# Strassen for the memory's values, with a summation tree, later hand-overs and gate tiles that leave the ring, in a one-core hybrid decoder layer

## The chip, the cores and the metric

The kernel runs on one core of one Trainium2 chip. The metric is the device time of one execution in microseconds (us). The engines are TensorE (PE, matrix products, with its weight loads listed as PEld), VectorE (DVE), ScalarE (ACT), GpSimd (POOL) and SyncE (SP), whose queue issues most of the DMAs. All weights come from HBM as float32 and the whole kernel keeps near-float32 accuracy.

## The reference

One layer works on x (256 tokens, width 2048) and a memory of 256 tokens:

```python
mem_h = rms_norm(mem, mem_norm_g)
x = x + hybrid_mixer(rms_norm(x, mix_norm_g), w_in, w_pool, ...)          # pooling heads and gated DeltaNet heads
x = x + memory_cross_attention(rms_norm(x, xa_norm_g), mem_h, w_xq, w_xkv, w_xo)
x = x + conv_glu_ffn(rms_norm(x, ffn_norm_g), w_gate, w_up, ...)          # width 5632
return rms_norm(x, final_norm_g)

def memory_cross_attention(h, mem_h, w_xq, w_xkv, w_xo):
    q = (h @ w_xq).reshape(B, S, XA_HEADS, XA_HEAD_DIM)
    kv = mem_h @ w_xkv                       # k: first 2048 columns, v: the other 2048
    s = einsum('bshd,bmhd->bhsm', q, k) * XA_HEAD_DIM ** -0.5
    o = einsum('bhsm,bmhd->bshd', softmax(s), v)
    return o @ w_xo
```

Inside the mixer, eight DeltaNet heads need per-token decays: the cumulative sums of g = -exp(a_log) * softplus(a + dt_bias), where a and b are 16 columns of the in-projection, scaled by the norm of x. The layer weights w_in, w_xkv, w_gate and so on are all 2048 rows deep, that is 16 tiles of 128 ("k tiles").

## The kernel before

**Products.** Every float32 operand is held as a pair: hi, a rounding that PE takes at full rate, and lo, the rest. One product of a weight tile with an activation tile is three matmuls, hi by hi, lo by hi and hi by lo. Weights come in raw tiles of 1 MB through a pool of three buffers (`load_raw`, tag raw, L110). Each raw tile is split in halves of 128x1024: a cast on ACT makes hi (L101), a subtraction on DVE makes lo (L102). The halves live in four buffers each (tags whi, wlo).

**Stages.** In the order of the program: the in-projection with the mixer's small products woven in; the keys of the memory (kk, w_k, 16 gemms); its values (pvs, w_v); the mixer's output (mix, w_mix); the queries (xq) with the attention; its output (xo); the feed-forward, whose gate and up products are done by Strassen's scheme in Winograd's form, on 11 blocks of four quarter products with 11 kinds of steps ("11", "22", "p1", "s3", ...); the down product; the last norm.

**Side lanes.** `job(lane, generator)` puts work in a lane; `pump` at set places of a gemm runs one step of a lane, up to the next `yield`; `drain` runs it to its end. So a `yield` is where PE goes on with gemm matmuls before the lane's next instruction. The lane "dn" first runs `decays`: it sums the logits (bc), transposes them (lps), scales them by the norm of x (rxps is the column sum of the squares xsum), makes gg, then gps (cumulative sums by matmul) and, in four quarters q, gm, its split gh and gl, and dps, the matmul whose exponential is the decay matrix Dm. The lane "dp" runs the four head pairs p (qp, w and others).

**The values.** `KV` holds keys and values. For each of four column groups n of 512, and for each of 16 k tiles, the memory's two token halves m_ (stationary mT, 128x128) are multiplied with the weight half (128x512 moving), three matmuls each, into two PSUM banks named pvs (L679 to L695). ACT scales the banks by the memory's norm rm on the way out.

**Gate and up.** `load`, `prepare`, `multiply` and `combine` (L979 on) work one step each: load one 512 KB tile, into the pool wr of eight buffers or, for the kind "11", into the SBUF region `ring`; split it; multiply; and combine PSUM banks. The load of "11" needs ring's space, which other tiles hold until the last xo product. A DMA on POOL's queue adds a second quarter onto the "11" tile, to give the sums s1, s2 and s4. While the first block runs, the lane "xr" transposes x (xtp) and writes it to DRAM (xt, xspill on SP's queue).

**Residual.** xres, x in its transposed form, is loaded in two DMAs of 1 MB (L703) and added to the mix banks (L706, L707).

**What sets the order.** A scheduler orders instructions on each engine by their place in the text and their priorities; the tiles of a pool decide when a load may be issued; a call of `seq` fixes the order of the instructions in it to that of the text.

## Time and profile before

| | |
|---|---|
| median of 3 runs | 1532.48 us (1530.06 to 1536.34) |
| profiled execution | 1533.36 us, of which the span is 1531.6 us |
| mean clock granted to PE | 0.992 |
| PE busy | 1490.8 us, 97% of the span, 7722 matmuls |
| DVE busy | 1099.3 us, 72% |
| ACT busy | 856.4 us, 56% |
| POOL busy | 221.5 us, 14% |
| chain that ended last | PE 82%, DVE 7%, DMA 4% |

The stages begin, in us of the span, at about: kk 313, values 412, mix 500, queries 588, attention output 705, gate and up 797, down 1275. Matmuls are pipelined, so the durations of neighbouring rows overlap, and the distance of their starts is what one costs. A number in brackets at the end of a row of a timeline is the idle time of the engine before the row and what ended it. PEclk is the granted clock of PE as a share of full speed.

### The profile page before, as it was taken

Reading aid. Unit: us, or ns where it says so; the run is one execution under the profiler, and the core shown is the slowest. Engines: PE = TensorE matmul, PEld = TensorE weight load, DVE = VectorE, ACT = ScalarE, POOL = GpSimd, SP = SyncE. Lnnn points to the kernel's source line nnn. Section 1 sums busy time; section 2 is a strip of 40 time slices with the busy share of each in tenths; the row PEclk is TensorE's granted clock in tenths of the full one; section 3 lists DMA queues with packets and bytes.
Section 4 is the critical chain, followed back from the end, with each engine's and each line's share of the span. In section 5 each row is a group of like instructions: output and inputs, shape, how many; then the busy total and the mean of one; then the engine's idle time right before and its main releaser. Section 6 shows DMA issues by size and latency. Waiting matters only on the chain.

```text
span 1531.6 us, 20542 instructions
## 1 busy us (share of the span) xinstructions
PE 1490.8 (97%) x7722; PEld 1261.1 (82%) x7722; DVE 1099.3 (72%) x1435; ACT 856.4 (56%) x1247; POOL 221.5 (14%) x237
## 2 busy tenths in 40 slices
PE   7899999999999999999988999999999999999997
PEld 4788889888888888998877888888888888888885
DVE  6978887676544676666756898898999998455445
ACT  5555656554444544555545666666666666444433
POOL 0442532441100121000320000000000000000000
PEclk9999999999999999999999999999999999999999
DMA  6445443457555555344539888888888879755651
GB/s 225 155 176 176 151 170 126 141 173 268 190 176 190 192 191 192 138 140 163 193 129 339 248 256 261 260 256 268 269 270 242 244 217 365 249 194 191 197 188 55
DMA packets 73715, 314.95 MB, mean 206 GB/s; under 512 B 12048, under 2 KB 12432, under 8 KB 57488
## 3 DMA queue, kind: packets, MB, share of 16 engines
q1 hardware_dynamic: 67136, 290.05, 54.1%
q0 software_dynamic: 6336, 23.07, 8.4%
q8 instruction: 60, 0.98, 0.2%
q10 hardware_dynamic: 144, 0.52, 0.1%
q14 instruction: 39, 0.32, 0.1%
HBM read 304.05 MB, written 9.57 MB: 205 GB/s over the span
## 4 chain that ended last, share of the span: by engine, by line
PE 82%; DVE 7%; DMA 4%; ACT 2%; POOL 2%; issue 1%; SPq 1%; POOLq 0%; ACTq 0%; DVEq 0%
PE b L882 9%; PE b L884 9%; PE b L883 9%; PE acc L1096 5%; PE acc L1095 5%; PE acc L1094 5%; PE xq L143 4%; PE xo L143 4%; PE mix L143 4%; PE kk L143 3%; PE pvs L691 2%; PE pvs L690 2%; PE pvs L689 2%; PE xq L144 2%; PE xo L144 2%; PE mix L144 2%
## 5 line engine op out<-in xcount | busy, mean ns | idle before, releaser
L960 ACT CAST wh<-wr 128x1024 fp32r<-128x1024 f32 x154 | 160.2, 1050 | 82.4 <-DVE wr L996 30.0
L961 DVE TENSOR_TENSOR wl<-wr,wh 128x1024 fp32r<-128x1024 f32 x154 | 185.2, 1219 | 27.1 <-ACT wh L960 26.0
L882 PE MATMUL b<-wh,hP 128*128 128x512 f32 x484 | 192.4, 398 | 8.0 <-ACT wh L960 5.5
L884 PE MATMUL b<-wh,hP 128*128 128x512 f32 x484 | 191.8, 397 | 0.0
L883 PE MATMUL b<-wl,hP 128*128 128x512 f32 x484 | 190.6, 394 | 1.0 <-DVE wl L961 1.0
L961 DVE TENSOR_TENSOR wl<-wd,wh 128x1024 fp32r<-128x1024 f32 x88 | 107.5, 1224 | 101.9 <-ACT wh L960 100.3
L960 ACT CAST wh<-wd 128x1024 fp32r<-128x1024 f32 x88 | 92.7, 1054 | 118.5 <-PE acc L1096 115.7
L961 DVE TENSOR_TENSOR wl<-ring,wh 128x1024 fp32r<-128x1024 f32 x88 | 106.5, 1220 | 31.9 <-ACT wh L960 31.8
L960 ACT CAST wh<-ring 128x1024 fp32r<-128x1024 f32 x88 | 91.5, 1051 | 63.5 <-PE b L884 24.8
L1094 PE MATMUL acc<-wh,aring 128*128 128x512 f32 x320 | 124.5, 389 | 0.0
L1095 PE MATMUL acc<-wl,aring 128*128 128x512 f32 x320 | 124.5, 389 | 0.0
L1096 PE MATMUL acc<-wh,aring 128*128 128x512 f32 x320 | 124.5, 389 | 0.0
L882 PEld LDWEIGHTS b<-wh,hP 128*128 128x128 f32 x484 | 91.9, 190 | 28.0 <-ACT wh L960 5.8
L102 DVE TENSOR_TENSOR wil<-wi,wih 128x1024 fp32r<-128x1024 f32 x78 | 100.3, 1293 | 16.1 <-ACT wih L101 15.8
L883 PEld LDWEIGHTS b<-wl,hP 128*128 128x128 f32 x484 | 91.9, 190 | 20.3 <-DVE wl L961 1.9
L884 PEld LDWEIGHTS b<-wh,hP 128*128 128x128 f32 x484 | 91.8, 190 | 18.8
L993 POOL DMA_DIRECT2D ring<-in_w_gu x44 | 38.5, 879 | 422.2 <-DVE sg L932 343.1
L101 ACT CAST wih<-wi 128x1024 fp32r<-128x1024 f32 x78 | 81.4, 1048 | 18.0 <-DMA wi<-in_w_in 6.3
L143 PE MATMUL xq<-h2T,wqh 128*128 128x512 f32 x240 | 84.9, 393 | 0.0
L143 PE MATMUL kk<-mT,wkh 128*128 128x512 f32 x240 | 84.4, 393 | 0.0
L143 PE MATMUL xo<-oT,woh 128*128 128x512 f32 x240 | 84.3, 392 | 0.0
L143 PE MATMUL mix<-yT,wmh 128*128 128x512 f32 x240 | 84.1, 392 | 0.0
(466 smaller groups left out, 3769.9 us busy)
## 6 DMA issues: line engine op xcount, KB each, us to landing
wr<-in_w_gu SPq DMA_DIRECT2D x156, 512.0 KB, 7.0
wd<-in_w_down SPq DMA_DIRECT2D x88, 512.0 KB, 4.8
wi<-in_w_in SPq DMA_DIRECT2D x39, 1024.0 KB, 5.0
ring<-in_w_gu POOLq DMA_DIRECT2D x44, 512.0 KB, 7.4
wk<-in_w_k SPq DMA_DIRECT2D x16, 1024.0 KB, 4.9
wv<-in_w_v SPq DMA_DIRECT2D x16, 1024.0 KB, 4.8
wm<-in_w_mix SPq DMA_DIRECT2D x16, 1024.0 KB, 4.9
wq<-in_w_xq SPq DMA_DIRECT2D x16, 1024.0 KB, 4.9
```

What stands on the lines that cost most here:

```text
L101: act.copy(hi, src)
L102: return dve.tensor_tensor(lo, src, hi.bitcast(F32), ALU.subtract)
L143: pe.matmul(ps, h, full, start=kk == 0, stop=False)
L144: i = pe.matmul(ps[:, T:], l, xt[:, 0, :], start=False, stop=False)
L882: pe.matmul(ps, xh, wh, start=first and i == 0, stop=False, skip_group_check=True)
L883: pe.matmul(ps, xh, wl, start=False, stop=False, skip_group_check=True)
L884: m = pe.matmul(ps, xl, wh, start=False, stop=last and i == 1, skip_group_check=True)
L960: cast[:] = [put(act.copy(h, src))]
L961: less[:] = [put(dve.tensor_tensor(l, src, h.bitcast(F32), ALU.subtract))]
L1094: pe.matmul(acc[t, n], ah, wh, start=first, stop=False)
L1095: pe.matmul(acc[t, n], ah, wl, start=False, stop=False)
L1096: return pe.matmul(acc[t, n], al, wh, start=False, stop=last)
```

## The change

It has five parts. The sum of x's squares is made by a tree of additions right behind the squares, in place of one reduction in the lane dn. Three hand-overs come later: dps yields 3, 2, 2 and 4 times in its four quarters in place of twice, and w of the first pair once more. The memory's sums for Strassen (`memory_sums`) are made in a lane during the K gemms 8 to 15, for half of the k tiles against the other half. The values are made by Strassen's scheme on column pairs c, in an order of steps that `seq` fixes in the text, with u and l tiles that serve two products each. In the feed-forward, the "11" tiles of the first block b = 0 come through the pool wr.

```diff
-            with tc.issue_after(last_split[0].ins):
-                dve.tensor_reduce(xsum, xsq.rearrange("p k t -> p t k"), AX.X, ALU.add)
+        for c in range(1, 4):
+            dve.tensor_tensor(xsq[:, 0:4], xsq[:, 0:4], xsq[:, 4 * c:4 * c + 4], ALU.add)
+        dve.tensor_tensor(xsq[:, 0:2], xsq[:, 0:2], xsq[:, 2:4], ALU.add)
+        dve.tensor_tensor(xsum, xsq[:, 0], xsq[:, 1], ALU.add)
...
-                yield
-                yield
+                for _ in range((3, 2, 2, 4)[q]):
+                    yield
                 dps = psd.tile([P, 512], F32, name="dps", tag="d")
...
+            if p == 0:
+                yield
             yield from more(2)
             w1 = psd.tile([P, 2, P], F32, name="w1", tag="d")
...
+        def memory_sums():
+            for g in range(2):
+                ...
+                dve.tensor_tensor(am, mg[:, :, 0].bitcast(F32), mg[:, :, 1].bitcast(F32), ALU.add)
+                yield
+                dve.tensor_tensor(s5, a21, a22, ALU.subtract)
+                dve.tensor_tensor(s7, a11, a21, ALU.subtract)
+                yield
+                dve.tensor_tensor(s6, a11, s5, ALU.subtract)
+                dve.tensor_tensor(s3, a12, s6, ALU.subtract)
+                yield
+                split(hi, lo, tmp[:, 1])
+                yield
...
+            up = ((("b3", A11), ("b2", A21)), (("b3", A12), ("b2", A22)))
+            low = ((("b1", A11), ("b7", A21)), (("b1", A12), ("b7", A22)))
+            one = lambda *u: (u, u)
+            KINDS = (("11", one(("b1", A11))), ("22", one(("b3", S3))), ("s1", one(("b5", S5))), ("u2", up),
+                     ("s3", one(("b7", S7))), ("u3", up), ("s2", one(("b6", S6))), ("21", one(("b1", A12))),
+                     ("l2", low), ("l3", low), ("s4", one(("b7", A22))))
+            loads = [(c, kind) for c in range(2) for kind in ("11", "22", "12", "u2", "u3", "21", "l2", "l3")]
...
+            def prepare(c, kind, h, uses):
+                two = slice(2 * h, 2 * h + 2)
+                ...
+                hi = st.tile([P, 2, 512], F32R, name="wvh", tag="whi", bufs=4)
+                lo = st.tile([P, 2, 512], F32R, name="wvl", tag="wlo", bufs=4)
+                seq(act.copy(hi, s))
+                seq(dve.tensor_tensor(lo, s, hi.bitcast(F32), ALU.subtract))
+                ready[c, kind, h] = hi, lo
+                if kind == "22":
+                    ...
+                    seq(dve.tensor_tensor(T4[c][:, two], raw[c, "11"][:, two], raw[c, "12"][:, two], ALU.add))
+                if kind == "s1":
+                    r = raw[c, "12"][:, two]
+                    seq(dve.tensor_tensor(r, r, raw[c, "22"][:, two], ALU.add))
+                if kind == "u2":
+                    r = T4[c][:, two]
+                    seq(dve.tensor_tensor(r, r, raw[c, "22"][:, two], ALU.add))
+                if kind == "s2":
+                    nc.gpsimd.dma_start(s, a["w_v"][2 * c, h][:, 2:4], accum_op=ALU.add)
...
+            AHEAD, NS, nl = 3, 22, 0
+            for s in range(-AHEAD, len(steps)):
+                while nl < len(loads) and due[loads[nl]] <= s + AHEAD + 10:
+                    fetch(*loads[nl])
+                    nl += 1
+                if s + AHEAD < len(steps):
+                    prepare(*steps[s + AHEAD])
+                if s < 0:
+                    continue
+                if s == NS + 1:
+                    last_part(0)
+                combine(s // NS, s % NS)
+                multiply(*steps[s])
+            last_part(1)
...
+            if f == 8:
+                for lane in ("dn", "dp", "pool"):
+                    drain(lane)
+                job("ms", memory_sums())
...
-        if kind == "11":
+        if kind == "11" and b:
             r = ring[:, 2 * (b % 2) + j].rearrange("p (i c) -> p i c", i=2)
         else:
             r = fp.tile([P, 2, 512], F32, name="wr", tag="wr", bufs=8)
```

`multiply` runs, for each use of a step's half tile, six matmuls of 128x512 (two k tiles by three); a step of the kinds u2, u3, l2 and l3 has two uses, one of the others one. `combine` and `last_part` form the values from the banks b1 to b7 with three DVE sums at step 14, three ACT scalings at 16, two DVE sums at 18, one ACT copy at 21, and one DVE sum behind the pair's end. `fetch` loads a u or l tile in one DMA of 1 MB and the others in two of 512 KB.

The first place is DVE's start: the splits of the first in_k weights (w0l, wil), the logits (bc), the sum of squares (xsum) and the norm (rxms). Before:

```order
L102 TENSOR_TENSOR w0l<-w_79,w0h 128x1024
L268 TENSOR_TENSOR bc<-bps,bc 16x256
L102 TENSOR_TENSOR wil<-wi,wih 128x1024 x2
L276 TENSOR_REDUCE xsum<-xsq 128x256
L102 TENSOR_TENSOR wil<-wi,wih 128x1024
L171 TENSOR_SCALAR rxms<-rxps 128x2
```

And now:

```order
L102 TENSOR_TENSOR w0l<-w_79,w0h 128x1024
L252 TENSOR_TENSOR xsq<-xsq 128x1024 x2
L272 TENSOR_TENSOR bc<-bps,bc 16x256
L252 TENSOR_TENSOR xsq<-xsq 128x1024
L253 TENSOR_TENSOR xsq<-xsq 128x512
L255 TENSOR_TENSOR xsum<-xsq 128x256
L102 TENSOR_TENSOR wil<-wi,wih 128x1024 x4
L171 TENSOR_SCALAR rxms<-rxps 128x2
```

The sum moved from behind two wil splits to before the first of them, and bc stands inside it.

The second place is SP's queue from the K weights (wk) over the values (wv), the mixer's output (wm), the queries (wq) and the attention's output (wo) to the first gate tiles (wr, ring), with the loads of xres and the writes of x (xspill). Before:

```order
L110 DMA wk<-in_w_k 128x2048 x9
L703 DMA xres<-in_xT 128x2048 x2
L110 DMA wk<-in_w_k 128x2048 x7
L110 DMA wv<-in_w_v 128x2048 x16
L110 DMA wm<-in_w_mix 128x2048 x16
L110 DMA wq<-in_w_xq 128x2048 x16
L110 DMA wo<-in_w_xo 128x2048 x16
L987 DMA ring<-in_w_gu 128x1024 x2
L987 DMA wr<-in_w_gu 128x1024 x10
L899 DMA xspill<-xt 128x512
```

And now, where the loads of the values at L743 are halves of 512 KB and those at L110 whole tiles (the middle of them left out):

```order
L110 DMA wk<-in_w_k 128x2048 x16
L743 DMA wv<-in_w_v 128x1024 x6
L110 DMA wv<-in_w_v 128x2048 x2
L743 DMA wv<-in_w_v 128x1024 x2
...
L110 DMA wm<-in_w_mix 128x2048 x4
L847 DMA xres<-in_xT 128x2048 x2
L110 DMA wm<-in_w_mix 128x2048 x12
L110 DMA wq<-in_w_xq 128x2048 x16
L110 DMA wo<-in_w_xo 128x2048 x16
L1131 DMA wr<-in_w_gu 128x1024 x9
L1131 DMA ring<-in_w_gu 128x1024
```

xres moved behind all of the values' loads, and the first gate tiles are wr's.

The third place is DVE at the start of the values: wvl are splits, vsum the sum of the tiles 11 and 12 (wv_4328 and wv_4334), wv_4331 the tile 22, wv_4337 the tile u2, km the last of the K gemms. Before, splits alone stood here; now:

```order
L759 TENSOR_TENSOR vsum_4353<-wv_4328,wv_4334 128x1024
L160 TENSOR_TENSOR km_4325<-kk_4290,kc_4323 128x256
L754 TENSOR_TENSOR wvl_4356<-wv_4331,wvh_4355 128x1024
L759 TENSOR_TENSOR vsum_4353<-wv_4328,wv_4334 128x1024
L754 TENSOR_TENSOR wvl_4371<-vsum_4353,wvh_4370 128x1024
L762 TENSOR_TENSOR wv_4334<-wv_4334,wv_4331 128x1024
L754 TENSOR_TENSOR wvl_4382<-vsum_4353,wvh_4381 128x1024
L762 TENSOR_TENSOR wv_4334<-wv_4334,wv_4331 128x1024
L754 TENSOR_TENSOR wvl_4396<-wv_4337,wvh_4395 128x1024
```

The second of the vsum rows from 11 and 12 is the last reader of the tile 11, and it stands behind the second split of 22 (wvl_4356); the first split of u2 (wvl_4396) is the last row.

## Rows read from the trace of the kernel before

**Rows 1.** The page, busy time by engine, share of the span, instructions.

```profile
PE 1490.8 (97%) x7722; PEld 1261.1 (82%) x7722; DVE 1099.3 (72%) x1435; ACT 856.4 (56%) x1247; POOL 221.5 (14%) x237
```

**Rows 2.** Waits of PE: line, releaser, us in total, times, longest us.

```profile
PE dps L324 <- ACT gh L101: 2.7, 3, 1.8
...
PE b L883 <- DVE wl L961: 1.0, 2, 0.5
```

**Rows 3.** Timeline of PE, 20 to 36 us: start, duration, [idle before <-releaser].

```profile
23.34 0.51 PE L143 MATMUL in_k<-hT,wih 128*128 128x512 f32 x1 [1.07 <-ACT wih L101]
24.60 0.58 PE L144 MATMUL in_k<-hT,wil 128*128 128x256 f32 x1 [0.75 <-DVE wil L102]
...
33.18 0.58 PE L166 MATMUL rxps<-cst,xsum 128*128 128x1 f32 x4 [0.81 <-DVE xsum L276]
34.22 0.39 PE L144 MATMUL in_k<-hT,wil 128*128 128x256 f32 x1 [0.46 <-DVE wil L102]
```

**Rows 4.** Busy time by windows; after POOL: PEclk, DMA share, GB/s.

```profile
25.00:28.00 3.00, 3.00 (x11) 2.52 (x11) 3.00 (x2) 1.96 (x2) 0.00 (x0) 0.51 0.85 289
33.00:40.00 7.00, 6.36 (x28) 5.57 (x29) 5.04 (x7) 1.69 (x4) 1.62 (x1) 0.76 0.51 177
797.00:804.00 7.00, 6.53 (x21) 4.70 (x22) 6.24 (x7) 5.88 (x8) 3.03 (x3) 0.59 1.00 351
840.00:844.00 4.00, 4.00 (x13) 3.10 (x12) 2.52 (x3) 2.11 (x3) 0.00 (x0) 0.57 1.03 410
```

**Rows 5.** Timeline of PE, the other idle places before it.

```profile
55.79 0.40 PE L311 MATMUL gps<-gg,cst 128*128 128x16 f32 x2 [1.94 <-DVE gg L304]
...
72.87 0.50 PE L324 MATMUL dps<-gh,mgr 128*128 128x512 f32 x1 [1.78 <-ACT gh L101]
...
153.10 1.13 PE L423 MATMUL qp<-Z,C 128*128 128x128 f32 x8 [2.50 <-DVE Z L418]
...
194.08 0.46 PE L529 MATMUL w<-R,Yall 128*128 128x128 f32 x2 [1.41 <-DVE R L522]
...
796.89 0.79 PE L882 MATMUL b<-wh,hP 128*128 128x512 f32 x1 [5.50 <-ACT wh L960]
...
808.46 0.66 PE L896 MATMUL xtp<-cst,xres 128*128 128x128 f32 x4 [1.66 <-ACT xt L898]
...
839.08 0.50 PE L882 MATMUL b<-wh,hP 128*128 128x512 f32 x1 [2.45 <-DVE ring L1019]
```

**Rows 6.** Timeline of DVE, 17 to 36 us.

```profile
19.93 0.41 DVE L268 TENSOR_TENSOR bc<-bps,bc 16x256 f32<-16x256 f32 x1 [2.07 <-ACT bc L267]
23.32 2.36 DVE L102 TENSOR_TENSOR wil<-wi,wih 128x1024 fp32r<-128x1024 f32 x2 [2.98 <-ACT wih L101]
25.59 7.44 DVE L276 TENSOR_REDUCE xsum<-xsq 128x256 f32<-128x4096 f32 x1
```

**Rows 7.** Timeline of PE in the values, seven steps from first to last.

```profile
439.77 0.39 PE L690 MATMUL pvs<-wvl,mT 128*128 128x512 f32 x1
...
441.40 0.40 PE L691 MATMUL pvs<-wvh,mT 128*128 128x512 f32 x1
```

**Rows 8.** Busy time by windows, K gemms and values: PE, PEld, DVE, ACT, POOL.

```profile
313.00:412.00 99.00, 98.64 (x573) 86.54 (x571) 64.25 (x90) 48.52 (x79) 25.47 (x28) 1.00 0.59 213
412.00:500.00 88.00, 88.00 (x380) 70.86 (x379) 39.42 (x33) 38.66 (x41) 0.00 (x0) 1.00 0.55 191
```

**Rows 9.** The tile wv: durations in ns (min, median, max), landing of its loads.

```profile
L101 ACT CAST wvh<-wv x32: 1035/1047/1057, 401.2 to 488.0; 128x1024 fp32r<-128x1024 f32 x32
L102 DVE TENSOR_TENSOR wvl<-wv,wvh x32: 1219/1224/1445, 402.3 to 489.1; 128x1024 fp32r<-128x1024 f32 x32
...
DMA to landing us min/median/max: 4.7/4.8/5.3
```

**Rows 10.** The tile xres: landing of its two loads.

```profile
DMA to landing us min/median/max: 7.9/9.0/10.1
```

**Rows 11.** Waits on SP's queue: line, releaser, us in total, times, longest us.

```profile
SPq L987 <- PE xo L141: 25.0, 1, 25.0
```

More of the change, by code (lines that the diff above doesn't have):

```diff
@@ L667, in hybrid_trunk @@
         mT = mbox[0]
+        mS = []
+        def memory_sums():
+            for g in range(2):
+                tmp = dn.tile([P, 2, 4, T], F32, name="mtmp", tag="kall", bufs=1)
+                if g:
+                    pair = dn.tile([P, 2, 4, T], F32R, name="mS1", tag="Yall", bufs=1)
+                    hi, lo = pair[:, 0], pair[:, 1]
+                else:
+                    hi, lo = (dn.tile([P, 4, T], F32R, name=n, tag="u4", bufs=2) for n in ("mSh", "mSl"))
+                mS.append((hi, lo))
+                am, ss = tmp[:, 0], tmp[:, 1].rearrange("p w (k t) -> p w k t", k=2)
+                mg = mT[:, 4 * g:4 * g + 4]
+                dve.tensor_tensor(am, mg[:, :, 0].bitcast(F32), mg[:, :, 1].bitcast(F32), ALU.add)
+                yield
+                a11, a12, a21, a22 = (am[:, k:k + 2, t * P:(t + 1) * P] for t in range(2) for k in (0, 2))
+                s5, s6, s7, s3 = (ss[:, w] for w in range(4))
+                dve.tensor_tensor(s5, a21, a22, ALU.subtract)
[6 more added lines that the diff above has]
+                yield
@@ L676, in hybrid_trunk @@
                 drain("mem")
+            if f == 8:
+                for lane in ("dn", "dp", "pool"):
+                    drain(lane)
+                job("ms", memory_sums())
             m = evac(ps, "k")
             pool.tensor_tensor(Kt[:, f, :], m, rmb, ALU.mult)
-        for n in range(4):
-            pvs = [psd.tile([P, 512], F32, name="pvs", tag="d") for _ in range(2)]
-            for kg in range(4):
-                raw = load_raw(a["w_v"][n, kg], [P, 4, 512], "wv")
-                gr = wsplit(raw, 2, "wv")
-                for k in range(4):
-                    kt = kg * 4 + k
-                    h, l = gr[k // 2][0][:, k % 2, :], gr[k // 2][1][:, k % 2, :]
-                    for m_ in range(2):
-                        s = slice(m_ * P, (m_ + 1) * P)
-                        pe.matmul(pvs[m_], mT[:, kt, 0, s], h, start=kt == 0, stop=False)
-                        pe.matmul(pvs[m_], mT[:, kt, 0, s], l, start=False, stop=False)
-                        i = pe.matmul(pvs[m_], mT[:, kt, 1, s], h, start=False, stop=kt == KT - 1)
-                    if kt % 2 == 1:
-                        pump(i)
-            for m_ in range(2):
-                act.activation(Vt[:, m_, n * 512:(n + 1) * 512], pvs[m_], AF.Copy, scale=rm[:, m_:m_ + 1])
+        drain("ms")
+        values()
         drain("dn")
```

73 lines of the change are left out of this document (added).

## The prediction

> **What bounds the kernel now.** I read the page first: TensorE (PE) is busy for 1490.8 of 1531.6 us, 97%, and DVE for 72% [rows 1]. So time falls only if PE gets fewer matmuls or loses less than the some 41 us that it stands idle or the extra that it spends at half clock. Next I read the list of what PE waited for: dps 2.7 us in three pieces, splits of gate weights (wl) 1.0 in two [rows 2]; none of the values' matmuls is in that list. Then the timeline of PE gave the other pieces where the change works: the sum of x's squares (rxps 0.81), gps 1.94, qp 2.50, w 1.41, and the entrance to the gate products, 5.50 for the first weight tile, 1.66 and 2.45 soon after [rows 3, 5]. A table by windows gave the granted clock behind them: 0.76 of full speed from 33 to 40 us, after the rxps wait, 0.59 for 7 us after the first gate tile, 0.57 for 4 us after the 2.45 [rows 4]. Full speed is the 2.4 GHz level; between that and 1 a window mixes it with 1.2 GHz. The profiled execution took 1533.36 us, 0.88 above the median 1532.48 and 1.76 beyond its span; the sum is made against it.
>
> **The sum of squares.** Before, one reduction of 128x4096 on DVE takes 7.44 us from 25.59, between the splits of the second weight tiles of in_k, and PE waits 0.81 for it at 33.18 and 0.46 for the split behind it at 34.22 [rows 3, 6]. The tree is three sums of 128x1024 (1.22 each, the median of a split of that shape [rows 9]), one of 512 (0.6, an estimate between its neighbours) and one of 256 (0.41 for 16x256, bc's row): 3.66+0.6+0.41 = 4.7 us. It stands before those splits, and DVE idles there 2.07 before 19.93 and 2.98 before 23.32, which is 5.05 in all [rows 6]: it fits, just. The two waits go, 1.27, and with them the slow stretch, 24% of the 7 us from 33 to 40, 1.7 [rows 4]. Together -3.0. If the tree ends a microsecond late, the 1.07 and 0.75 waits before it [rows 3] grow by that: bounds -3 to 0.
>
> **Hand-overs.** The dps matmuls come one step later in the first and two in the last quarter; they waited 2.7 for ACT's gh, the largest piece 1.78 before the last quarter [rows 2, 5], and PE has other gemm work in those steps, so about -2.7 at best; since the delay moves the later parts of the lane by three steps, some other wait may grow: -3 to -1. The w matmul of the first pair waited 1.41, and one step more takes it out: -1.4 [rows 5]. gps and qp, which waited 1.94 and 2.50 [rows 5], are moved against their producers by nothing that I can price: 0, bounds -2 to +3 by the larger of them.
>
> **Values, the work.** Before: 2 halves x 4 columns x 16 k x 3 = 384 matmuls of 128x512. They start every 0.233 us (439.77 to 441.40, seven intervals [rows 7]; the 392 to 399 ns of the group's rows overlap). After, per column pair 8 half-k kinds use one product (11, 22, s1, s3, s2, 21, s4) or two (u2, u3, l2, l3), 15 uses x 2 halves x 6 matmuls = 180, and two pairs: 360. That is -24 x 0.233 = -5.6 us. In exchange DVE gets 12 more splits at 1.22, 12 sums at about 1.22 and some ten combines of 128x512 at 0.6 to 0.7, together some 36 us, in a stage where it was busy 39.4 of 88 [rows 8]: it has room. ACT's 12 casts of 1.05 too.
>
> **Values, the waits.** The rows cannot show this, so I walk it through. A weight tile of 1 MB takes 4.7 to 5.3 us from issue to landing, median 4.8 [rows 9], and there are three raw buffers. Before, a tile lasted PE 24 x 0.233 = 5.6 us and two were ahead, so PE was never idle here, 88.0 busy of 88.0 [rows 8]. Now 11, 22 and 12 hold all three from the start, as each is needed for sums, and u2's load stands on SP behind the last sum 11+12. A single step is 6 x 0.233 = 1.40, a double one 2.80. Let 0 be PE's first step. The last split of 22 takes a wh buffer that the K gemm frees at 0, so cast 1.05, split 1.22 and sum 1.22 [rows 9] end at 3.5. u2 lands at 8.3 to 8.6, is cast by 9.6 and split by 10.8. PE wants it after six steps, at 8.4: it waits 1.2 for the cast and 0.9 for the split. u3 takes the buffer that u2 leaves at 13.1, lands at about 18 and is split at 20.3; PE wants it at 18.9: 1.1 more. The second pair has the same order, its sum about 0.6 later: 2.7 and 1.1. Together 2.1+1.1+2.7+1.1 = 7.0 us of new waits; bounds 0 (loads early or the buffer free sooner) and 14 (each tile late by its whole 4.8, less what lies between).
>
> Behind a wait the clock may fall. Of the waits of 1.4 us and over before, 2.50 and 2.45 were followed by slow stretches [rows 4, 5]; 1.94, 1.78, 1.66 and 1.41 were not. A stretch costs some 43% of 4 us, 1.7. I take two stretches and let half of the second be hidden in the next wait, +2.0; bounds 0 and 6.8. So the stage comes to -5.6+7.0+2.0 = +3.4. [...]
>
> **Sums for the memory, and xres.** The sums of the memory's tiles run in the K gemms f 8 to 15 on DVE, 8 us in a stage where DVE was busy 64 of 99 [rows 8]: 0, bounds 0 to 1. xres's two loads leave SP's queue behind wk's ninth and go behind wm's fourth, waiting for the values' last step; they take 7.9 to 10.1 us [rows 10] and the first residual can be late by some 16 us before a PSUM bank is missed (three of the 16 mix gemms, which last 88 us): 0, bounds 0 to +3.
>
> **Entrance to the gate.** Before, the first tiles go into the ring, whose space is free only when the last xo matmul is done; SP waited 25.0 us for it and issued the loads behind it [rows 11]. PE lost 5.50 until the cast, then 41% of 7 us, 2.9, to the clock; 1.0 for two splits; later 1.66 and 2.45, and 43% of 4, 1.7 [rows 2, 4, 5]: 15.2 in all. After, the first loads wait only for splits on DVE some 18 us earlier, so they land before xo ends. But the first gate product now takes the PSUM bank of the last xo gemm, and must wait for the second residual add of f 15, which stands behind a split on DVE: 0.4 for the matmul to end, two adds of 0.41 with a split of 1.22 between them, 2.4 us. Then one slow stretch, 1.7, and in the first block, where xt has two buffers and each waits for its spill's DMA in a full queue, waits such as 1.66, 2.45 and a split's 0.5 remain; I take 4.3 for them. Together 8.4 for 15.2: -6.8; bounds -11 (only 4.2 left) and 0 (the later tiles come as late as before, since the DMA engines were full, shares 1.00 and 1.03, in both windows there [rows 4]).
>
> **Sum.** -3.0-2.7-1.4+0+3.4+0-6.8 = -10.5: 1533.4-10.5 = 1522.9, against medians some 1522 to 1523.
>
> **The rivals.** (a) The values don't wait: loads land before they are wanted, as they did before. Against it: the chain sum, load, cast, split is 10.8 long and PE is there at 8.4. Then -5.6 in place of +3.4: 1514. (b) The entrance keeps its loss: the wait for the ring's space is replaced by that for the bank, and with the DMAs full to 844 every later tile arrives as before; only the stage at the start gains: 1533.4-7.1+3.4 = 1530. For it are the shares 1.00 and 1.03 [rows 4]; against it that the first 4 MB leave 18 us earlier. (c) Slower: in the values each wait for u2 and u3 lets the clock fall, and it stays at half through the double tile, 24 x 0.233 = 5.6 us more for each of the four, 22.4 in place of 2.0. That gives 1543. It decides if a wait of 1.1 us is enough to drop the clock and it comes back only after the tile. For it: 1.07 and 0.75 at 23 us were followed by 0.51 for 3 us [rows 3, 4]; against it: 1.94 and 1.78 were not followed by any.
>
> **How the numbers follow.** Forecast 0.53, its own range 1517 to 1529; (a) 0.13; (b) 0.21; (c) 0.13. A measurement of this kernel can tell about 0.5%, 7.7 us, from no change. Faster than 1524.8: two thirds of the forecast's chance, 0.35, and (a)'s 0.13, 0.48. Same: the rest of the forecast, 0.18, and (b), 0.39 less 0.01. Slower: (c), with a little of (b): 0.14. The range takes in (a)'s side and (b), and half of what lies to (c): 1512 to 1537.
>
> **What would show it.** In the profile after: no reduction of 7.44 us and no wait at rxps; dps not in PE's list, w shorter; 360 pvs matmuls; in that stage PE waits for the cast and split of the u tiles, four places, 7 us; first gate matmul some 2.4 us after the last of xo, waiting for DVE's residual. Wrong, if the values show no wait (a), if the clock is low through them (c), or if PE loses some 15 us between the end of xo and 54 us later (b).

## The result, and the profile after

The change is slower: 1544.34 us (1542.29 to 1544.89, 6 runs) against 1535.11 us for the kernel before in the same six rounds, ratio 1.0064 with a 95% interval of 1.0049 to 1.0079. The profiled execution has a span of 1542.6 us, 11.0 more than before.

The page of the kernel after, busy time by engine. To be read beside [rows 1]: PE has 24 matmuls less and 2.7 us less to do, and yet the span is longer, so PE waits some 14 us more.

```profile
PE 1488.1 (96%) x7698; PEld 1256.4 (81%) x7698; DVE 1136.5 (74%) x1487; ACT 871.6 (57%) x1263; POOL 221.8 (14%) x241
```

Where the time went is told by the first start of each stage's matmuls, from the rows of the tiles (us). By the same rows the attention's output begins at 696.1 in the kernel before, and the down product at 1280.0, not at about 705 and 1275.

| stage | before | after | length before | length after |
|---|---|---|---|---|
| in_k to its end | 13.3 to 77.7 | 11.6 to 74.7 | 64.4 | 63.1 |
| from there to the first kk | 315.2 | 323.5 | 237.5 | 248.8 |
| kk | 409.4 | 418.3 | 94.2 | 94.8 |
| values (pvs) | 499.0 | 512.4 | 89.6 | 94.1 |
| mix, queries, xo to the last xo | 791.0 | 804.3 | 292.0 | 291.9 |
| to the first gt (block 0 of gate and up) | 857.8 | 868.9 | 66.8 | 64.6 |
| from there to the first down product | 1280.0 | 1291.0 | 422.2 | 422.1 |

Two stages got longer: the second half of the mixer by 11.3 us, where the prediction had a gain, and the values by 4.5, where it had a loss of 3.4. The first gate block, where it had its largest gain, won 2.2.

The list of PE's waits after (line, releaser, us in total, times, longest us). rmpb, pool, ops, in_u and the second qp row are new against the list of before; dps is down from 2.7 [rows 2] to 0.8, with 0.5 more for gl, and the xsum row is gone, as forecast.

```profile
...
PE pvs L782 <- DVE wvl L754: 3.7, 5, 1.2
PE gps L313 <- DVE gg L306: 3.0, 1, 3.0
PE rmpb L180 <- DVE rmdg L177: 2.8, 1, 2.8
PE qp L425 <- DVE Z L420: 2.7, 1, 2.7
PE xtp L1040 <- ACT xt L1042: 2.5, 2, 1.6
PE b L1026 <- DVE ring L1163: 2.4, 1, 2.4
PE b L1026 <- DVE xres L851: 2.4, 1, 2.4
PE pool L143 <- DVE Dm L481: 2.1, 1, 2.1
PE qp L425 <- POOL C L418: 1.8, 1, 1.8
PE pvs L781 <- ACT wvh L753: 1.8, 2, 1.2
PE b L1026 <- ACT wh L1104: 1.7, 1, 1.7
PE ops L541 <- DVE vs L536: 1.6, 1, 1.6
PE in_u L144 <- DVE wil L102: 1.6, 1, 1.6
...
PE dps L326 <- ACT gh L101: 0.8, 1, 0.8
```

The timeline of DVE after, 286 to 315 us (start, duration, in brackets the idle time before and what ended it), shows where three of these come from. mt is the pooled mean of a feature tile; it waits for pB, POOL's shifted sums. Each time something that PE needs stands behind it on DVE's queue: vs for ops, two sums of the lane and a wil split for in_u, Dm for the pool product.

```profile
286.80 0.43 DVE L604 SCALAR_TENSOR_TENSOR mt<-pB,pA 128x256 f32<-128x256 f32 x1 [2.05 <-POOL pB L600]
...
287.23 0.35 DVE L536 TENSOR_SCALAR vs<-w,sbA 128x128 f32<-128x128 f32 x1
...
303.70 0.42 DVE L604 SCALAR_TENSOR_TENSOR mt<-pB,pA 128x256 f32<-128x256 f32 x1 [2.99 <-POOL pB L600]
...
305.00 1.22 DVE L102 TENSOR_TENSOR wil<-wi,wih 128x1024 fp32r<-128x1024 f32 x1
...
313.39 0.43 DVE L604 SCALAR_TENSOR_TENSOR mt<-pB,pA 128x256 f32<-128x256 f32 x1 [2.77 <-POOL pB L600]
...
313.81 0.69 DVE L481 TENSOR_TENSOR Dm<-raw_kq,Dm 128x512 f32<-128x512 f32 x1
```

In the kernel before the same waits stand in the timeline of DVE at 300 to 309 us, but what is behind them there (a split that was early, vs at 309) was not yet wanted:

```profile
300.66 0.43 DVE L600 SCALAR_TENSOR_TENSOR mt<-pB,pA 128x256 f32<-128x256 f32 x1 [1.35 <-POOL pB L596]
...
308.86 0.42 DVE L600 SCALAR_TENSOR_TENSOR mt<-pB,pA 128x256 f32<-128x256 f32 x1 [2.77 <-POOL pB L596]
```

rmpb is a matmul of the memory's norm: it wants DVE's rmdg, which wants POOL's rmr, which wants DVE's rmms. In the timeline of DVE after, rmms stands right behind f, an operation of the lane that waits for POOL, and the two pieces of rmdg take 1.48 us, beside C, an operation of the lane that the timeline of POOL has at that time:

```profile
221.72 0.16 DVE L550 TENSOR_TENSOR f<-sq__2299 128x4 f32<-128x4 f32 x1 [1.06 <-POOL sq__2299 L476]
221.80 0.16 DVE L171 TENSOR_SCALAR rmms<-msum 128x2 f32<-128x2 f32 x1
222.77 1.48 DVE L177 TENSOR_SCALAR rmdg<-cst,rmr 128x128 f32<-128x128 f32 x2 [0.81 <-POOL rmr L172]
```

```profile
222.71 1.26 POOL L418 TENSOR_TENSOR C<-U,cst 128x512 f32<-128x512 f32 x1
```

In the timeline of DVE before, no wait stands in front of rmms and rmdg takes 0.48, so 1.0 to 1.1 us each of rmpb's 2.80 come from these two neighbours:

```profile
226.32 0.13 DVE L171 TENSOR_SCALAR rmms<-msum 128x2 f32<-128x2 f32 x1
227.26 0.48 DVE L177 TENSOR_SCALAR rmdg<-cst,rmr 128x128 f32<-128x128 f32 x2 [0.81 <-POOL rmr L172]
```

In the values, the timeline of PE after shows the wait for u2 of the first column pair, and the slow matmuls behind it: starts 0.43 apart in place of 0.23 [rows 7], seven times up to 433.4, which is the 1.2 GHz level. It is the only slow stretch of that stage.

```profile
428.53 0.49 PE L781 MATMUL pvs<-wvh,mT 128*128 128x512 f32 x1 [1.21 <-ACT wvh L753]
429.79 0.49 PE L782 MATMUL pvs<-wvl,mT 128*128 128x512 f32 x1 [0.77 <-DVE wvl L754]
...
430.44 0.63 PE L781 MATMUL pvs<-wvh,mT 128*128 128x512 f32 x1
430.87 0.63 PE L782 MATMUL pvs<-wvl,mT 128*128 128x512 f32 x1
```

Between the starts 428.53 and 429.79 lie 1.26 us, where 0.23 is normal; the row names 0.77 as idle. So this wait cost 0.26 more than the bracket says, and some 0.1 at the next matmul; the others of the stage cost 0.16 to 0.27 more, and the same 0.1 where no second wait followed. The stage is 360 x 0.233 = 84 us of matmuls, nine waits of 6.0 us together, 2.5 for their restarts, and 1.6 for the slow stretch: the measured 94.1.

### The profile page after: what moved, and what is told of

Its sections match the earlier page's. It is cut to its first block, busy times and chain, and to the rows that moved or that the text cites. A ratio compares the mean times of both kernels' runs of the same rounds, so it can differ in the third digit from the quotient of the medians.

```text
span 1542.6 us, 20613 instructions
## 1 busy us (share of the span) xinstructions
PE 1488.1 (96%) x7698; PEld 1256.4 (81%) x7698; DVE 1136.5 (74%) x1487; ACT 871.6 (57%) x1263; POOL 221.8 (14%) x241
## 4 chain that ended last, share of the span: by engine, by line
PE 79%; DVE 9%; DMA 4%; ACT 3%; POOL 3%; issue 2%; SPq 0%; DVEq 0%; POOLq 0%; ACTq 0%
PE b L1026 9%; PE b L1027 9%; PE b L1028 9%; PE acc L1238 5%; PE acc L1239 5%; PE acc L1240 5%; PE xq L143 4%; PE kk L143 4%; PE mix L143 4%; PE xo L143 3%; DVE wil L102 2%; PE xq L144 2%; PE kk L144 2%; PE mix L144 2%; PE xo L144 2%
## 5 line engine op out<-in xcount | busy, mean ns | idle before, releaser
L1105 DVE TENSOR_TENSOR wl<-wr,wh 128x1024 fp32r<-128x1024 f32 x162 | 194.8, 1221 | 38.3 <-ACT wh L1104 36.4
L1104 ACT CAST wh<-wr 128x1024 fp32r<-128x1024 f32 x162 | 168.2, 1050 | 81.8 <-PE b L1028 32.0
L1104 ACT CAST wh<-ring 128x1024 fp32r<-128x1024 f32 x80 | 83.3, 1051 | 54.1 <-PE b L1028 29.7
L1105 DVE TENSOR_TENSOR wl<-ring,wh 128x1024 fp32r<-128x1024 f32 x80 | 96.9, 1221 | 21.0 <-ACT wh L1104 21.0
L1137 POOL DMA_DIRECT2D ring<-in_w_gu x40 | 34.8, 870 | 403.3 <-DVE sg L1076 350.7
```

The costliest lines, as they stand in the source:

```text
L1104: cast[:] = [put(act.copy(h, src))]
L1105: less[:] = [put(dve.tensor_tensor(l, src, h.bitcast(F32), ALU.subtract))]
```

## Experiments

The times are medians; ratios are to the kernel before on the same chip in the same rounds, with their 95% intervals. "In_k's end to pvs" is the length from the last in_k matmul to the first of the values, 331.7 us before and 343.6 after: it leaves out how the first loads of an execution fall. The kernel before had medians from 1533.58 to 1535.11 us in the rounds of this section and of the result, so a difference between medians of different rounds is good to some 1.5 us.

**The hand-overs taken out.**

```diff
-                for _ in range((3, 2, 2, 4)[q]):
-                    yield
+                yield
+                yield
...
-            if p == 0:
-                yield
```

> The changed kernel with the hand-overs as before (dps two steps, w no extra one); tree, values and gate entrance stay. Five new idle times of PE stand between 224 and 315 us of the changed kernel (rmpb 2.80, qp 1.80, ops 1.62, in_u 1.61, pool 2.07, together 9.9), and kk starts 8.3 us later than before. Theory H, the three added steps move the whole DeltaNet lane against the gemms and so make them: they go, kk starts at about 315 (the dps waits of 2.7 come back), time about 1536. Rival T, the tree makes them, since the lane begins earlier: they stay, kk starts at 323 to 326, time 1544 to 1547. Rival V, the values' loads and early drain make them: they stay here too.

1534.5 us, ratio 0.9999 (0.9987 to 1.0010), 9.8 below the change. The five waits are gone and in_k's end to pvs is 332.0. Theory H held, V fell.

**The reduction back, the new hand-overs kept.** Edit: the tree's five lines out, tensor_reduce back in the lane.

> The changed kernel with the sum of squares by one reduction as before, the new hand-overs kept. Theory H: the waits between 224 and 315 us stay, and the 3 us won in the first 75 us are lost: about 1547. Rival T: the waits go, kk starts at about 316, time about 1537.

1549.67 us, ratio 1.0099 (1.0077 to 1.0120); all five waits are there, in_k's end to pvs is 345.4. T fell: the tree is worth 5 us to the change.

**Both as before.**

> The changed kernel with both the reduction and the hand-overs as before; values and gate entrance new. Theories H and T: the start is that of before, kk starts at 315.2, the values cost 4.5 us more and the gate's entrance 2.2 less, so about 2 to 3 us above the kernel before. Rival V: the waits between 224 and 315 us stay, about 10 us above.

1538.04 us, ratio 1.0025 (1.0012 to 1.0037), 3.8 above the kernel before where 2 to 3 were expected; in_k's end to pvs 332.5. Against no_handovers, the tree alone is worth 3.5 us (0.26% of ratio, good to about 0.17).

**The values as before, all else as in the change.** Edit: `values()` and `memory_sums()` out, the loop of before back; the early drain of the lanes and the late load of xres go with them.

> The changed kernel with the values as before (no sums for the memory, no early drain, xres loaded early). Theories H and T: the start keeps its waits, kk starts at 323 or so, and only the 4.5 us of the values' stage come back: about 1540. Rival V: the waits between 224 and 315 us go with the values: about 1530.

1538.43 us, ratio 1.0032 (1.0019 to 1.0044): 5.9 below the change, and the waits of the mixer stay. So the new values cost 5 to 6 us.

**The hand-overs one at a time.** The dps steps alone, then the step before w alone, both on the change without the other.

> The changed kernel with the dps hand-overs of the change (3, 2, 2, 4 steps) but without the extra step before w of the first pair. Theory H1, the three dps steps shift the DeltaNet lane and make the waits at rmpb, qp, ops, in_u and pool between 224 and 315 us: they stay, kk starts at about 323 or later (w's 1.4 comes back), time about 1545. Rival H2, the step before w makes them: they go, kk starts at about 313, time about 1534.

> The changed kernel with two steps before each dps as before and the extra step before w of the first pair. Theory H1: no waits between 224 and 315 us, w's 1.41 at 191 us goes, kk starts at about 311, time 1533. Rival H2: the waits are there, kk starts at about 321, time 1544.

dps_only took 1535.31 us, ratio 1.0007 (0.9998 to 1.0016); w_only 1542.91, ratio 1.0056 (1.0039 to 1.0073). By the times H2 held: the one step before w makes nearly all of the loss. The profiles, one execution each, are less simple. In_k's end to pvs is 334.8 with the dps steps, 336.4 with the step of w, 343.6 with both. The first pvs matmul itself starts at 407.5 us without the steps, and then at 409.0, 414.8 and 418.3, which follows the times better; but that counts in_k too, which took 66.9 us in the execution of w_only and 62.0 in that of no_handovers. And the waits that w_only has are, but for 1.89 at rmpb, others (w 2.57 and 1.33 at 328 to 330 us, qp 1.56 and 1.14) than those of the change. So no single place holds the loss; which waits come depends on both shifts.

**The step of w, taken back later in the same lane.** On the change with two steps before each dps:

```diff
-            for _ in range(5):
+            for _ in range(4 if p == 0 else 5):
                 yield
             otp = pt("otp")
```

> The changed kernel with two steps before each dps as before and the extra step before w of the first pair, but four steps in place of five before otp of the first pair, so that all later pairs stand where they did without it. Theory A, the step costs by its shift of the later lane work against the other queues, not by itself: the waits of 161 to 331 us of the kernel with the w step alone (qp 1.56 and 1.14, rmpb 1.89, w 2.57 and 1.33) go, pvs starts at about 406 and the time is about 1533. Rival A2, the step itself or the first pair makes them: pvs starts at about 414, 1542.

1535.18 us, ratio 1.0008 (0.9999 to 1.0017); in_k's end to pvs is 331.9. The step itself neither costs nor wins: w's wait of 1.41 is gone, qp waits of 0.50 and 1.14 came. What costs is that all later pairs stand one step later. Theory A held.

**The pooled means later on DVE's queue.** On the change with all its hand-overs; the three operations of mt become a job in the pool lane, one step behind POOL's sums, and `pool_out` yields once less at its start (condensed):

```diff
-                dve.scalar_tensor_tensor(mt, src[:, 16:], 1.0 / w, A[:, 16:], ALU.mult, ALU.subtract)
-                ...
-                split(mx[c][:, 0, :], mx[c][:, 1, :], mt)
+                job("pool", pool_mean(n, mx[c], src, A))    # yields once, then the same operations
```

> The changed kernel with all its hand-overs, but the three DVE operations that make the pooled mean (mt, m16) moved from the text of the gemm into a step of the pool lane, so that they are issued on DVE one step behind POOL's sums pB for which they wait. Theory Q, DVE's queue in order is the cause: vs, wil and Dm, for which PE waits (ops 1.62, in_u 1.61, pool 2.07), stand on DVE right behind mt, which waits 2.05, 2.99 and 2.77 for pB. Then these three waits go and kk starts some 5 to 6 us earlier, at 317 or 318; time about 1539. Rival Q2, POOL or ACT itself is late: the waits stay or others of the same size come, kk starts at about 323, time 1544.

1539.97 us, ratio 1.0040 (1.0027 to 1.0052): 4.4 below the change, 3.7 by the ratios. The waits at pool and qp (POOL's C) are gone, in_u fell from 1.61 to 0.88, ops only from 1.62 to 1.40, rmpb kept its 2.81. The timeline of DVE in this kernel shows why ops stayed: one of the mean's operations still waits for pB right in front of vs.

```profile
281.80 0.17 DVE L589 TENSOR_TENSOR m<-pB,cst 128x16 f32<-128x16 f32 x1 [2.05 <-POOL pB L610]
281.89 0.60 DVE L536 TENSOR_SCALAR vs<-w,sbA 128x128 f32<-128x128 f32 x2
```

Theory Q is shown for the part that moved: taking mt out of the way gives 4.6 of the 11.9 us back (in_k's end to pvs 339.0). For rmpb mt is not the cause.

**The values' steps in another order.** Without the hand-overs; u2 and u3 come right behind 11, so that the buffers are not held by tiles that wait to be summed (the lines are condensed).

```diff
-            KINDS = (11, 22, s1, u2, s3, u3, s2, 21, l2, l3, s4)   # each with its uses
+            KINDS = (11, u2, u3, 22, s1, s3, s2, 21, l2, l3, s4)
-            loads: 11, 22, 12, u2, u3, 21, l2, l3
+            loads: 11, u2, u3, 22, 12, 21, l2, l3
```

> The changed kernel without the new hand-overs, and with the values' steps in the order 11, u2, u3, 22, s1, s3, s2, ... (loads in the order 11, u2, u3, 22, 12, 21, l2, l3; the sum 11+12 moves to s1, the sum with 22 to s3), so that the three raw buffers first hold tiles that no sum keeps. Theory S, the values' stage of 94.1 us is 84 of matmuls plus some 10 of waits for the u tiles (1.35, 0.76, 1.25, 0.49, 0.76, 0.76 and two of 0.24, each with some 0.37 of restart behind it, and one slow stretch of 1.9), because u2's load waits for the buffer of 11: the waits for u2 and u3 go, the stage takes 84.5 to 86, time about 1526 (8 to 9 us below the same kernel with the order of the change). Rival S2, the extra DVE work (sums, combines) makes them: the stage stays at 92 to 94, time about 1534.

1535.44 us, ratio 1.0009 (0.9998 to 1.0020): nothing won. The waits for u2 and u3 are gone, and the stage still takes 94.3 us. The timeline of PE in this kernel shows a wait at every step from s1 to s3, 2.27 us apart:

```profile
427.24 0.50 PE L780 MATMUL pvs<-wvl,mS 128*128 128x512 f32 x1 [0.77 <-DVE wvl L756]
429.51 0.50 PE L780 MATMUL pvs<-wvl,mSh 128*128 128x512 f32 x1 [0.60 <-DVE wvl L756]
431.78 0.51 PE L780 MATMUL pvs<-wvl,mS 128*128 128x512 f32 x1 [0.61 <-DVE wvl L756]
```

and that of DVE what fills them, a split and a sum for each step, starts 1.14 apart:

```profile
427.10 1.22 DVE L760 TENSOR_TENSOR wv<-wv 128x1024 f32<-128x1024 f32 x1
428.24 1.22 DVE L756 TENSOR_TENSOR wvl<-wv,wvh 128x1024 fp32r<-128x1024 f32 x1
429.37 1.22 DVE L763 TENSOR_TENSOR vsum<-vsum,wv 128x1024 f32<-128x1024 f32 x1
430.51 1.22 DVE L756 TENSOR_TENSOR wvl<-wv,wvh 128x1024 fp32r<-128x1024 f32 x1
```

S2 held for what is left: with the loads in time, DVE has 2.28 us of work for each 1.40 us of matmuls there. The combines add waits of 1.31 and 1.15.

**Other PSUM banks.** On the reordered kernel; the pool of the gemms gets b6 in place of b7, so that the last xo product lies in another bank than the first gate product's.

```diff
-                        pool_, tag = (psg, "g") if name in ("b7", "b2") else (psd, "d")
+                        pool_, tag = (psg, "g") if name in ("b6", "b2") else (psd, "d")
```

> As the reordered kernel, with b6 in place of b7 in the PSUM pool of the gemms, so that the last xo gemm no longer lies in the bank that the first gate product takes. Theory B, PE's 2.44 us at the first gate product come from that bank alone: the wait goes, PE starts right behind xo, and the time is 2 to 3 us below the reordered kernel, about 1523. Rival B2, the later tiles of the first block come as late as before, so that what is won at the first product is lost in the next 40 us: no difference within 0.5 us.

1534.65 us, ratio 1.0004 (0.9993 to 1.0014), 0.8 below reordered: no difference that can be told. PE starts the gate at once (791.4 to 791.6), but from the last xo to the first gt it takes 65.4 us for 66.5. Of the 2.4 us of the first product 1.1 are left at that point, and the times show none for certain: nearer to B2 than to B.

**One sum on POOL.** On the kernel with other banks; 11+12 is made by POOL, in the step of 22.

```diff
-  seq(dve.tensor_tensor(T4[c][:, two], raw[c, "11"][:, two], raw[c, "12"][:, two], ALU.add))
+  seq(pool.tensor_tensor(T4[c][:, two], raw[c, "11"][:, two], raw[c, "12"][:, two], ALU.add))
```

> As the kernel with reordered values and other banks, with the sum 11+12 made by POOL in the step of 22 in place of DVE in that of s1. The reordered values took 94.1 us although the loads come in time: PE waits 0.6 (and some 0.3 of restart) for the split in each of the steps 22 to s3, 2.27 us apart, which is two DVE operations of 1.14 each to 1.40 us of matmuls. Theory D, DVE is what bounds those steps: with one sum less the waits shrink by two thirds or more and the stage takes 85 to 88 us, time about 1528. Rival D2, POOL's adds, some 2.5 us each, are late in their place: the stage stays at 92 to 96.

1536.9 us, ratio 1.0022 (1.0012 to 1.0033), stage 94.0 us: D2. The timeline of POOL and then that of DVE in this kernel: the two adds take 4.77 us, DVE idles for 3.97 until the sum is cast, and its split, which begins beside POOL's second add, lasts 2.33 in place of 1.22. The waits of some 0.6 in the steps are still there.

```profile
417.59 4.77 POOL L748 TENSOR_TENSOR vsum<-wv 128x1024 f32<-128x1024 f32 x2 [9.67 <-PE pvs L781]
```

```profile
421.11 2.33 DVE L756 TENSOR_TENSOR wvl<-vsum,wvh 128x1024 fp32r<-128x1024 f32 x1 [3.97 <-ACT wvh L755]
```

**No second loads in the first gate block.** On that kernel. Before and after, the loop issues the loads of the first p2 tiles twice; the first ones are never used.

```diff
-        if s + LOADS + AHEAD < len(plan) and s + AHEAD >= 0:
+        if s + LOADS + AHEAD < len(plan) and s >= 0:
             load(*plan[s + LOADS + AHEAD])
```

> As the kernel with the sum on POOL, without the second loads of the first block's p2 tiles (before, each of the two 512 KB tiles is loaded twice, the first time in vain). In all kernels so far the first block of the gate loses 10 to 15 us however early its first tile is, with the DMA engines full. Theory F, the first block is bound by what its DMAs bring: 1 MB less is worth 1 MB at some 400 KB per us, 2 to 3 us, in the stretch up to 50 us behind xo. Rival F2, the order of the queue counts and not the amount: 0 to 1 us.

1531.59 us, ratio 0.9980 (0.9970 to 0.9991), 5.3 below. From the last xo to the first gt it takes 61.6 us for 66.8. The gain that F named came, at twice its size; whether by F's reason is taken up below.

**The entrance alone, on the kernel before.**

```diff
-        if kind == "11":
+        if kind == "11" and b:
```

> The kernel before with one line changed: the first block's 11 tiles come through wr and not the ring. Theory F, the first block is bound by what its DMAs bring and the earlier first tile wins only what lies before the full stretch: PE starts at once behind xo (no wait of 5.5), but from the end of xo to the end of the gate products it takes 485 to 487 us for 488.7, time 2 to 3 us below before. Rival E, as predicted: about 7 us below, since no bank stands in the way here even 9.

1532.76 us, ratio 0.9986 (0.9975 to 0.9997): 0.5 to 3.8 us faster. PE starts the gate 0.2 us behind xo in place of 5.9, and has the first gt 66.6 us behind xo in place of 66.8. The last gate product starts 488.6 us behind xo for 488.7, where F had 485 to 487: in this profile nothing is left of the earlier start, and E fell.

**The duplicates out of the kernel before, nothing else.**

> The kernel before without the second loads of the first block's two p2 tiles; nothing else. Theory F, the first block is bound by its DMAs' bytes: 1 MB less gives 2 to 5 us in the 54 us behind xo, though the first tile still comes 5.5 us after xo: about 1530. Rival F2, only with the tiles out of the ring: no difference within 1 us.

1530.61 us, ratio 0.9983 (0.9973 to 0.9993), first gt 63.2 us behind xo, though the wait of 5.45 for the first tile is still there. The rows of the tile gt in three kernels (instruction, count, duration in ns, first and last start), to be read with the last xo at 792.5, 794.3 and 789.3: the entrance alone, no_duplicates, and this one.

```profile
L922 PE MATMUL gt<-cst,ring x88: 270/272/328, 859.1 to 1293.4; 128*128 128x128 f32 x88
```

```profile
L1064 PE MATMUL gt<-cst,ring x88: 270/272/328, 855.9 to 1290.5; 128*128 128x128 f32 x88
```

```profile
L922 PE MATMUL gt<-cst,ring x88: 270/272/328, 852.5 to 1286.8; 128*128 128x128 f32 x88
```

All three are 434.3 to 434.6 from first to last: what the first block loses is decided before its first gt. One execution differs from the next here: from the last xo to the first gt the thirteen kernels with the first tiles through wr and the second loads kept took 63.8 to 66.8 us, the five without the second loads 61.6 to 63.5.

That the second loads cost time is shown; that it is by their bytes is not. Each also takes one of the eight buffers of wr, and the next load into that buffer has to wait until it has landed. SP's list of waits has a row for it in the kernel before and, the second one here, in the one with the sum on POOL; without the second loads that wait is 1.0 us at most.

```profile
SPq L987 <- DMA wr<-in_w_gu: 9.2, 4, 4.4
```

```profile
SPq L1129 <- DMA wr<-in_w_gu: 3.4, 2, 2.6
```

No run parts the bytes from the buffers.

**Sums by DMA.** First 11+12 by an accumulating DMA, with 11 loaded into the sum's own buffer, on no_duplicates; then all sums so, with b7 copied early and the order u2, u3, 11, 22, s1, s3, 21, s2.

```diff
+                if kind == "11":
+                    nc.gpsimd.dma_start(s, a["w_v"][2 * c + 1, h][:, 0:2], accum_op=ALU.add)
```

> As no_duplicates, with the sum 11+12 made by a DMA on POOL's queue that adds 12 onto the tile of 11, which is loaded into the sum's buffer and not into one of the three raw ones. Theory D, DVE is what bounds the steps 22 to s3 when the loads are in time: DVE does four sums per column pair less the two... that is, two operations of 1.14 per half in s1 and s3 only, and the split of 22 and s1 goes ahead in the double steps; the stage takes 85 to 88 us and the time is about 1525. Rival D2, the 22 splits and sums simply stand too close for three steps ahead with four buffers: the waits in s1 and s3 stay, the stage takes 91 to 94, time about 1530.

> As sum_by_dma, with all sums of weight tiles made by accumulating DMAs on POOL's queue (six of 1 MB instead of two more than the change), the steps in the order u2, u3, 11, 22, s1, s3, 21, s2, l2, l3, s4, b7 copied by ACT before its bank is written again, and the combines two steps later. Theory D, what kept the stage at 92 to 94 us was DVE's sums beside its splits (each single step of 1.40 us held two DVE operations of 1.14): now one split per step is left, PE waits for less than 2 us and the stage takes 84 to 87 us, time about 1524. Rival X, something else (the DMAs' landing, four split buffers for steps of 1.4 us) takes their place: the stage takes 90 or more, time about 1531.

sum_by_dma: 1531.34 us, ratio 0.9982 (0.9970 to 0.9995), stage 92.8 us. The waits in s1 and s3 fell from four per column pair to one of 0.60; left are the last combine (1.06 and 1.20, DVE late) and 1.48 and 0.76 for the second pair's 11. So the waits went as in D, and the stage is as long as in D2. all_sums_by_dma: 1540.36, ratio 1.0034 (1.0022 to 1.0046), stage 102.6 us: X. Now PE waits for the DMAs. The landing row of its tile vsum (4 plain and 12 accumulating DMAs of 512 KB), and the two longest waits in the timeline of PE:

```profile
DMA to landing us min/median/max: 3.9/7.4/11.7
```

```profile
426.75 0.49 PE L779 MATMUL pvs<-wvh,mSh 128*128 128x512 f32 x1 [1.56 <-ACT wvh L757]
...
480.28 0.79 PE L779 MATMUL pvs<-wvh,mSh 128*128 128x512 f32 x1 [4.34 <-ACT wvh L757]
```

Each chain here is split, accumulate, land, cast and split again. The waits are not all: behind them the clock fell. The table by windows shows a granted clock of 0.62 from 426 to 434 us and 0.63 from 478 to 492 (third number from the end), and 0.90 over the stage, where the change had 0.98.

```profile
426.00:434.00 8.00, 4.75 (x9) 2.80 (x10) 3.27 (x3) 4.02 (x6) 1.53 (x2) 0.62 0.77 208
478.00:492.00 14.00, 10.79 (x28) 7.44 (x29) 8.12 (x7) 8.16 (x9) 1.75 (x2) 0.63 0.81 186
```

A version that reaches 84 us was not found.

**The version that the runs point to.** no_duplicates with the values of before; tree and gate tiles through wr stay, hand-overs as before.

> The kernel without duplicates of before's round (no_duplicates), with the values as in the kernel before: tree, gate tiles through wr and no second loads of p2 stay, hand-overs as before. If the 94 us of the reordered values against 89.6 are all that the values cost, it is 4 to 5 us below no_duplicates, about 1527; the gain of 5 at the first block stays.

1525.4 us (1523.83 to 1528.07), ratio 0.9944 (0.9929 to 0.9958): faster than both kernels, by 8.6 us than before. Its page, busy time by engine: the 7722 matmuls of before [rows 1], in a span of 1526.2 us.

```profile
PE 1489.4 (98%) x7722; PEld 1260.7 (83%) x7722; DVE 1097.3 (72%) x1439; ACT 856.4 (56%) x1247; POOL 221.0 (14%) x237
```

## Why the prediction was wrong

Forecast was about 1522.5 us, 10 below; measured is 9 above, outside the range.

- **The sum of squares: right.** Forecast -3.0; the runs give -3.5 (good to some 2.6) without and -5.3 with the new hand-overs. From 33 to 40 us the granted clock is 1.00 in place of 0.76. The waits 0.81 and 0.46 went; part came back at once at gps, which waits 3.0 for 1.94 [rows 5], since gg is not earlier by as much as PE; and the 4.1 us behind that wait ran at a granted clock of 0.58, where it was 1.00 before.
- **Hand-overs: the step that failed.** The prediction counted the waits that the added steps remove, -2.7 and -1.4. What they bring it took at 0, with bounds: for dps "some other wait may grow", by 1.7 at most, for gps and qp +3, the larger of two waits that were there. It looked only at how the lane moves "against their producers". It left out that a lane's instructions share DVE's and POOL's queues with the other lanes. Measured: +9.8 us in place of -4.1, though most of the waits at dps and w did go (0.8 and 0.5 are left at dps, 0.2 at w). One step in the first pair moves every later pair against the splits, the pooled means and the memory's norm; DVE's mt waits 14.3 us for POOL's pB over the mixer in the kernel before and 15.2 in the one after, but afterwards vs, wil and Dm are behind it. That the shift and not the step costs is shown by w_compensated, and mt's share of it by mean_later (3.7 to 4.4 us). For the rest no_handovers shows that the order of the lane is the cause. What in it, the rows show for two thirds of rmpb's 2.8, though no run takes f or C away from there; for what is left it stays open.
- **Values: right in sign and mechanism, short by 1 to 2.5 us.** Forecast +3.4, stage +4.5, time +5 to 6. The u tiles came late as walked through: PE waited 1.21 and 0.77 for u2, forecast 1.2 and 0.9, in the first pair; in the second 0.58 and 0.77 for u2 and 0.76 for u3, forecast 2.7 and 1.1. All waits came to 6.0 of the forecast 7.0, the slow stretch to 1.6 of 2.0. Not forecast were the restarts, 2.5 together, and, within the 6.0, waits at s1 (0.21 and 1.25) and at the combines (0.24 twice): -5.6+6.0+2.5+1.6 = +4.5. u3 of the first pair was split at 439.4 and PE came to it at 439.6; without the slow stretch PE would have come 1.6 earlier and waited. The prediction held DVE for free ("it has room") by the average of the stage; reordered shows that beside the single steps it has not.
- **The slow rival had the time right and not the cause.** (c) gave 1543, by half clock through four double tiles. One stretch of some nine matmuls was slow, 1.6 us, behind the waits for the first of those tiles. That the clock can stay at half for longer shows in all_sums_by_dma, behind waits of 1.27 to 4.34 us.
- **Entrance to the gate: first tile right, later waits mis-sized.** First tile early, 2.44 us of bank wait in place of 5.50, both as forecast. The term that failed is the 4.3 us for the later waits of the first block: they came to 8.1 (xtp 2.5, ring 2.4, wh 1.7, wl 1.5). Of -6.8, the first block won 2.2 in the profile, and the change at the gate alone 2.1 (0.5 to 3.8). Rival (b) was nearer: later tiles are as late as before (wh 1.66, wl 0.76 and 0.72 and ring 2.45 at 843 to 850 us), while the DMA engines are busy for 0.99 of the 54 us behind xo before and 0.93 after. The tables by windows of the kernel before and of the one after show PE busy for the same 43.4 and 43.5 us of these; what changed is the granted clock, 0.91 and 0.97, with ten more matmuls done.

```profile
791.00:845.00 54.00, 43.42 (x187) 33.87 (x186) 33.75 (x33) 30.14 (x38) 6.44 (x6) 0.91 0.99 333
```

```profile
804.30:858.30 54.00, 43.48 (x197) 34.06 (x196) 33.68 (x34) 27.95 (x37) 6.30 (x7) 0.97 0.93 277
```

  That the first product is not what binds shows in the run with other banks, which has kept 1.1 of its 2.4 us at the first gt and no certain gain in its time. What makes the later tiles late is shown in part: the second loads do, by their bytes or their buffers.
- **The sum.** By the ratios, and each part measured in another kernel: -4.0 (tree) +10.0 (hand-overs) +4.9 (values) -2.1 (entrance) = +8.8 us for the measured 9.8 (0.64%).

## What to carry to other kernels

A step added to one lane of a kernel with queues in order is not priced by the wait that it removes: list what then stands behind every long wait on the shared queues, or take the step back later in the same lane so that the rest keeps its place. A stage that is free on average can be bound step by step; count the operations of each engine beside each short step. And where the later tiles of a stretch come late with the DMA engines busy, an earlier first tile wins little (2 us here for 5.5 of waiting), while loads that nobody uses cost time (2.6 to 5.3 us here for two of 512 KB): look for those first.

## What the runs showed of the hardware that was not expected

A wait of PE of 0.77 us by the profile's bracket put 1.26 us between two starts that are normally 0.23 apart, and the next start came 0.33 later: 0.36 more than it shows. In the values of the changed and the reordered kernel the waits that no second one followed cost 0.26 to 0.38 more than they show.

A DVE split of 128x1024 that began beside POOL's add of that shape took 2.33 us in place of 1.22, in both column pairs of the kernel with the sum on POOL. Two DVE operations of 128x128 (rmdg) beside POOL's C of 128x512 took 1.48 us in place of 0.48.

In the kernel after, the four accumulating DMAs of 512 KB onto the sum's tile landed 8.8 to 12.5 us after their issue, where the plain loads of the same stage, 512 KB and 1 MB, took 3.7 to 8.1, and the plain 1 MB loads of the kernel before 4.7 to 5.3 [rows 9].
